# A two-layer encoder on one core: the loads, the transposes and the squares of the first twenty microseconds in another order

## The chip, the cores and the metric

The kernel runs on one core of a Trainium2 chip. The metric is the device time of one execution in microseconds. Three runs of the kernel before gave 854.73, 854.85 and 855.80 us; their median is 854.85 us.

## What is computed

The program is a trunk of two layers over one sequence of 256 tokens with 1024 channels, all in float32. A layer has two sub-layers with a residual sum after each.

```python
for layer in range(DEPTH):
    h = h + _token_mixer(_rmsnorm(h, norm1[layer]), w_in[layer], ...)   # pooling, attention, gates
    h = h + _conv_ffn(_rmsnorm(h, norm2[layer]), w_up[layer], ...)      # gated MLP
return _rmsnorm(h, norm_f)

def _rmsnorm(x, g):
    y = x * lax.rsqrt(jnp.mean(x * x, axis=-1, keepdims=True) + EPS)
    return y * g
```

The token mixer's first product is `xn @ w_in`; its columns hold among others the values `v` of three head groups, 512 columns each. The change touches only what comes before and during the product for the first 512 of these columns in the first layer.

## The kernel before, in words

**Products.** Each float32 operand is split into a high part (rounded to the multiplier's format) and a low part (the rest), and a product of two operands is made of three passes: high by high, low by high, high by low. Below, hh, lh and hl stand for these, with x's part named first and the weight's second. ScalarE makes the high part of a weight tile (`wh`), VectorE the low part (`wl`).

**The start (`begin_values_of_x`, L767 on).** x lies in the tile `h`, two tokens to a partition: t=0 holds the even tokens and t=1 the odd ones. For the values the kernel doesn't wait for the norm: the vector `norm1` is multiplied into the rows of the weights (`gcol`, one column for each chunk of 128 channels), and the factor of each token is multiplied onto the result later. So the first product needs `norm1` (loaded as 8 rows, `grows`, and turned by TensorE at L394), the raw chunks of x turned by TensorE (`turn_x`, L780 to L798), and the weights.

The contraction goes over 8 chunks of 128 channels, k=0 to 7, and there are two accumulators, t=0 and 1: 8 x 2 x 3 = 48 products (L839) in all, each 128 by 128 by 512. The weights come in two pieces of 1 MB, k=0 to 3 and k=4 to 7, the first loaded in four DMAs and the second in two. `split(k)` gives three closures that make the high part on ScalarE, the low part on VectorE, and (used for k=0 alone) the high part on VectorE (L261); `both(k)` issues the first two. The tiles for the parts of k=0 to 3 are named `m`, of k=4 and 5 `ybig`, of k=6 and 7 `at`. What `turn_x` leaves in PSUM (`xt_ps`) is cast on ScalarE to `xuh` (L793), and VectorE makes the rest `xul` (L794). `square(t, n)` sums the squares of one half of x's columns, n=0 on ScalarE (L804) and n=1 on VectorE (L808); GpSimd adds the two and raises the sum to the power -1/2 (L813 to L816), into `rstd`. `whole` (L822) adds both parts of x back together on VectorE.

**After it.** TensorE turns the two `rstd` columns into rows (`r_ps`, L908, placed behind the last of the 48 products), and goes on with the products of the next two value groups (L930), whose weights are `wh` and `wl`. From 41 us on come the long stages (L691).

**What sets the order.** Every engine works through its own list in the order in which the program's scheduler writes it; on the engines concerned this is the order of the code, save where the scheduler lets a later piece pass. SyncE issues nearly all loads. ScalarE's queue issues two DMAs at the start: `norm1` (L376) and the first quarter of x's odd tokens (L374); the other x loads and the weights are on SyncE's. Ahead of the first real work TensorE multiplies a constant tile by itself, to be busy (`warm`, widths in WARM, L37): six times 128 columns before L394, once 64 columns behind it, and once 64 columns behind the first transposes. GpSimd makes the identity for the transposes at its start.

Of the kernel before, what the change touches and what calls it, by code (L numbers as in the profile page):

```python
# [16 lines left out]
P = 128  # L17
# [16 lines left out]
NT = 5  # L34


WARM = ((P,) * 6, (P // 2,), (P // 2,))  # L37
POOLS = {("q", 1): (2, 2), ("k", 1): (0, 2)}
GROUPS = (("u", 1), ("u", 0), ("q", 0), ("k", 0), ("q", 2), ("k", 2), ("q", 1), ("k", 1))
NQ = NF // 4  # L40
# [240 lines left out]
def encoder(ctx, tc, x, w_in, w_pool, pool_scale, w_a, w_b, w_o, norm1, norm2, w_up, conv_w,  # L281
# [85 lines left out]
    def begin():  # L367


        rows8 = sm.tile([KD, P], F32, tag="gain", bufs=1, name="grows")  # L370
        first, second = W.load_by(4), W.load_by(2)

        def part_of_x(queue, t, cc):
            queue.dma_start(out=h[:, t, cc], in_=xv[:, t, cc])  # L374

        nc.scalar.dma_start(out=rows8, in_=norm1[0].rearrange("(k p) -> k p", p=P))  # L376
# [17 lines left out]
        nc.tensor.transpose(ps[:, 0:KD], rows8, ident[:KD, :KD])  # L394
        nc.vector.tensor_copy(gcol, ps[:, 0:KD])
        ps = mmp.tile([P, P], F32, tag="mm", name="warm_ps")
        warm(ps, ones, WARM[1])
        return lambda widths: warm(ps, ones, widths)

    def warm(ps, a, widths):  # L400

        for n in widths:
            nc.tensor.matmul(ps[:, 0:n], a, a[:, 0:n], start=True, stop=True)
# [363 lines left out]
    def begin_values_of_x():  # L767
# [32 lines left out]
        def square(t, n):  # L800
            cc = HALVES[n]
            junk = sm.tile([P, 512], F32, tag="p", bufs=3, name="junk")
            if n == 0:
                nc.scalar.activation(  # L804
                    junk, h[:, t, cc], AF.Square, scale=D**-0.5, accum_out=ss[t][:, n : n + 1]
                )
            else:
                nc.vector.scalar_tensor_tensor(  # L808
                    out=junk, in0=h[:, t, cc], scalar=1.0 / D, in1=h[:, t, cc],
                    op0=ALU.mult, op1=ALU.mult, accum_out=ss[t][:, n : n + 1],  # L810
                )
            if n == 0:
                nc.gpsimd.tensor_scalar_add(ss[t][:, 3:4], ss[t][:, 0:1], EPS)  # L813
            else:
                nc.gpsimd.tensor_add(out=ss[t][:, 3:4], in0=ss[t][:, 3:4], in1=ss[t][:, 1:2])
                return nc.gpsimd.tensor_tensor(out=rs[t], in0=ss[t][:, 3:4], in1=mhalf, op=ALU.pow)  # L816

        def whole(n, tag):

            ks = slice(4 * n, 4 * n + 4)  # L820
            f = big.tile([P, 4, 2, P], F32, tag=tag, name="xu")
            nc.vector.tensor_add(out=f, in0=xuh[:, ks].bitcast(F32), in1=xul[:, ks].bitcast(F32))  # L822
            return f
# [29 lines left out]
        every = ("hh", "lh", "hl")  # L853
        keep = [turn_x((t,), 0, 2) for t in range(2)]
        more(WARM[2])
        _, lo, hi = split(0)
        hi()
        for k in keep:
            k()
        lo()  # L860
        products((0, 0, ("hh",)), (1, 0, ("hh",)), (0, 0, ("lh",)), (1, 0, ("lh",)))
        keep = turn_x((0, 1), 2, 2)
        both(1)
        keep()
        products((0, 0, ("hl",)), (1, 0, ("hl",)))
        both(2)
        products((0, 1, ("hh", "lh")), (1, 1, ("hh", "lh")), (0, 1, ("hl",)), (1, 1, ("hl",)))
        both(3)
        square(0, 0)
        square(1, 0)  # L870
        square(0, 1)
        pool = square(1, 1)
        products((0, 2, ("hh", "lh")), (1, 2, ("hh", "lh")))
        keep = turn_x((0,), 4, 4)
        products((0, 2, ("hl",)), (1, 2, ("hl",)))
        keep()
        products((0, 3, every))
        keep = turn_x((1,), 4, 4)
        both(4)
        keep()  # L880
        W.load(5)
        products((1, 3, every), (0, 4, every))
        both(5)
        products((1, 4, every), (0, 5, every))
        f0 = whole(0, "q0")
        both(6)
        products((1, 5, every), (0, 6, every))
        both(7)
        products((1, 6, every), (0, 7, every))
        f1 = whole(1, "k0")  # L890
        pe = products((1, KD - 1, ("hh", "hl", "lh")))
        W.load(6)
        W.n_got = W.n_split
# [601 lines left out]
```

## Time and profile before

| what | value |
|---|---|
| median of three runs | 854.85 us |
| profiled execution, device time | 854.77 us |
| its span in the trace | 853.0 us |
| what lies around the span | 1.77 us |
| TensorE's busy time | 844.8 us of 853.0 |
| DMA | 214.03 MB, mean 251 GB/s |
| TensorE's first product of the 48 | at 5.73 us |
| TensorE's first pass of L691 | at 41.1 us |

All times inside the span count from its start. In the lists in order of time a row has the start, the length, the engine, the line, the operation, out<-in with sizes, the count of instructions that the row merges, and in brackets the idle time of that engine before it and who ended it. PE is TensorE, PEld its weight loads, DVE VectorE, ACT ScalarE, POOL GpSimd, SP SyncE; a q behind the name is the engine's queue. TensorE's matmuls overlap, so one that lasts 0.39 us can start 0.23 us behind the one before.

### The profile page before, as it was taken

How to read it: one execution, taken by the hardware profiler on the slowest of the kernel's cores; microseconds unless marked ns; L12 is line 12 of the kernel's file. 1: busy time of each engine (PE TensorE's matmuls, PEld its weight loads, DVE VectorE, ACT ScalarE, POOL GpSimd, SP SyncE). 2: the span in 40 equal slices, each digit the busy share in tenths (PEclk: the TensorE clock that was granted, in tenths of full speed). 3: DMA queues.
4: the chain of work that ended last, by engine and by line, in shares of the span. 5: the costliest groups of instructions: out<-in, count | busy, mean ns of one | idle time of the engine just before them, and what ended most of it. 6: DMA issues, size and time to landing. Idle time of an engine off the chain costs nothing.

```text
span 853.0 us, 11006 instructions
## 1 busy us (share of the span) xinstructions
PE 844.8 (99%) x3925; PEld 705.7 (83%) x3925; DVE 620.6 (73%) x885; ACT 490.5 (58%) x723; POOL 33.6 (4%) x96
## 2 busy tenths in 40 slices
PE   9999999999999999999999999999999999999997
PEld 7888888888888888888888888888888888888885
DVE  7958777757765976878655687868567767777774
ACT  7744566654543865657545454577454556556663
POOL 1700000000010000000000000000000100000000
PEclk9999999999999999999999999999999999999999
DMA  9699997895657879986726899868777489799941
GB/s 326 212 302 285 294 292 233 252 293 210 222 209 263 300 250 301 293 284 233 245 100 216 261 280 330 245 226 264 242 257 269 147 289 315 230 288 288 296 145 50
DMA packets 147678, 214.03 MB, mean 251 GB/s; under 512 B 7768, under 2 KB 68640, under 8 KB 147624
## 3 DMA queue, kind: packets, MB, share of 16 engines
q1 hardware_dynamic: 147320, 212.93, 76.8%
q8 instruction: 31, 0.51, 0.2%
q10 hardware_dynamic: 304, 0.40, 0.1%
q14 instruction: 23, 0.19, 0.1%
HBM read 186.02 MB, written 27.28 MB: 250 GB/s over the span
## 4 chain that ended last, share of the span: by engine, by line
PE 98%; DMA 1%; SPq 0%; DVE 0%; ACT 0%; issue 0%; DVEq 0%; ACTq 0%
PE t_ps L691 64%; PE v_ps L691 6%; PE res_ps L610 6%; PE res_ps L608 6%; PE res_ps L609 6%; PE v_ps L930 3%; PE pool_ps L595 1%; PE v_ps L839 1%; PE o_ps L1200 1%; PE s_ps L1152 1%; PE s_ps L1147 1%; PE o_ps L1196 1%; PE xt_ps L522 1%; DMA h<-in_x_dram 1%; PE xt_ps L787 0%; SPq L184 0%
## 5 line engine op out<-in xcount | busy, mean ns | idle before, releaser
L245 DVE TENSOR_TENSOR wl<-raw,wh 128x1024 fp32r<-128x1024 f32 x274 | 332.0, 1221 | 159.0 <-ACT wh L243 158.1
L691 PE MATMUL t_ps<-wh,x 128*128 128x512 f32 x1408 | 438.8, 390 | 0.0
L243 ACT CAST wh<-raw 128x1024 fp32r<-128x1024 f32 x274 | 286.3, 1052 | 211.5 <-PE t_ps L691 146.4
L691 PEld LDWEIGHTS t_ps<-wh,x 128*128 128x128 f32 x1408 | 264.3, 188 | 54.8
L691 PE MATMUL t_ps<-wl,x 128*128 128x512 f32 x704 | 273.9, 389 | 0.0
L691 PEld LDWEIGHTS t_ps<-wl,x 128*128 128x128 f32 x704 | 132.2, 188 | 27.3
L610 PE MATMUL res_ps<-wh,actk 128*128 128x512 f32 (+1 forms) x184 | 70.0, 380 | 0.0
L609 PE MATMUL res_ps<-wl,actq 128*128 128x512 f32 (+1 forms) x184 | 69.9, 380 | 0.0
L608 PE MATMUL res_ps<-wh,actq 128*128 128x512 f32 (+1 forms) x184 | 69.8, 380 | 0.0
L691 PE MATMUL t_ps<-wh,po 128*128 128x512 f32 x128 | 41.4, 395 | 0.0
L608 PEld LDWEIGHTS res_ps<-wh,actq 128*128 128x128 f32 x184 | 34.6, 188 | 6.6
L609 PEld LDWEIGHTS res_ps<-wl,actq 128*128 128x128 f32 x184 | 34.6, 188 | 6.6
L610 PEld LDWEIGHTS res_ps<-wh,actk 128*128 128x128 f32 x184 | 34.6, 188 | 6.6
L487 POOL TENSOR_SCALAR ss<-ss 128x1 f32<-128x1 f32 x8 | 2.2, 279 | 773.5 <-ACT junk L480 773.5
L691 PEld LDWEIGHTS t_ps<-wh,po 128*128 128x128 f32 x128 | 24.0, 188 | 4.9
L1373 ACT ACTIVATE y<-a,prm 128x256 f32<-128x256 f32 x44 | 26.5, 602 | 1.5
L608 PE MATMUL res_ps<-wh,m 128*128 128x512 f32 (+1 forms) x72 | 26.5, 368 | 0.0
L609 PE MATMUL res_ps<-wl,m 128*128 128x512 f32 (+1 forms) x72 | 26.3, 365 | 0.0
L741 DVE STREAM_TRANSPOSE crossing<-t_ps 128x512 f32<-128x512 f32 x40 | 26.2, 693 | 0.0
L610 PE MATMUL res_ps<-wh,m 128*128 128x512 f32 (+1 forms) x72 | 26.0, 366 | 0.0
L691 PE MATMUL v_ps<-wh,x 128*128 128x512 f32 x80 | 25.6, 392 | 0.0
L691 PE MATMUL t_ps<-wl,po 128*128 128x512 f32 x64 | 24.9, 390 | 0.0
(193 smaller groups left out, 931.1 us busy)
## 6 DMA issues: line engine op xcount, KB each, us to landing
raw<-in_w_in_dram SPq DMA_DIRECT2D x58, 1024.0 KB, 6.8
raw<-in_w_up_dram SPq DMA_DIRECT2D x40, 1024.0 KB, 7.1
raw<-in_w_down_dram SPq DMA_DIRECT2D x22, 1024.0 KB, 6.0
crossing<-crossing SPq DMA_DIRECT2D x22, 512.0 KB, 8.5
crossing<-way SPq DMA_DIRECT2D x16, 512.0 KB, 4.8
raw<-in_w_a_dram SPq DMA_DIRECT2D x8, 1024.0 KB, 5.1
raw<-in_w_o_dram SPq DMA_DIRECT2D x8, 1024.0 KB, 7.0
zga<-crossing SPq DMA_DIRECT2D x40, 128.0 KB, 3.7
```

Of the source, the lines that this page charges most:

```text
L243: inst = nc.scalar.copy(out=h, in_=src)
L245: inst = self.rests[i] = nc.vector.tensor_sub(out=l, in0=src, in1=h.bitcast(F32))
L522: nc.tensor.transpose(pt[:, k, :], xn[:, c0 : c0 + P], ident)
L595: nc.tensor.matmul(out, w(k), x, start=(steps is first and k == 0), stop=(steps is last and k == nk - 1), skip_group_check=turns["rest"],)
L608: nc.tensor.matmul(ps, ah, wh, start=first, stop=False, skip_group_check=on)
L609: nc.tensor.matmul(ps, ah, wl, start=False, stop=False, skip_group_check=on)
L610: nc.tensor.matmul(ps, al, wh, start=False, stop=last, skip_group_check=on)
L691: nc.tensor.matmul(ps, x2[:, 2 * n + j, part, t, :], w[:, j, :], start=(n + m == 0), stop=(n == last and m == 5),)
L741: nc.vector.transpose(out=y[:, t].rearrange("p q c j -> p c q j"), in_=rows[t])
L839: return nc.tensor.matmul(ps[t], a[:, k, t, :], w[:, k % 2, :], start=first, stop=last)
L930: nc.tensor.matmul(ps[t], a[:, k, t, :], w[:, j, :], start=(k + m == 0), stop=(k == KD - 1 and m == 2),)
L1373: nc.scalar.activation(y, a, AF.Identity, bias=b, scale=w1)
```

## The change

1. `norm1`'s 8 rows are loaded from GpSimd's queue, ahead of the identity, and no longer from ScalarE's. So the first quarter of x's odd tokens is the first DMA on ScalarE's queue.
2. The warming matmuls are seven of 128 columns before L394, none behind it, and one of 128 columns behind the first transposes.
3. The transposes of x's chunks k=2 and 3 stand behind hh and lh of k=1, and the order of the products, splits and later transposes is another.
4. All four squares are made on ScalarE, later than before: the first two behind the split of k=6, the other two behind that of k=7.

```diff
-WARM = ((P,) * 6, (P // 2,), (P // 2,))
+WARM = ((P,) * 7, (P,))
...
-        nc.scalar.dma_start(out=rows8, in_=norm1[0].rearrange("(k p) -> k p", p=P))
+        nc.gpsimd.dma_start(out=rows8, in_=norm1[0].rearrange("(k p) -> k p", p=P))
...
-        warm(ps, ones, WARM[1])
         return lambda widths: warm(ps, ones, widths)
...
-            if n == 0:
-                nc.scalar.activation(
-                    junk, h[:, t, cc], AF.Square, scale=D**-0.5, accum_out=ss[t][:, n : n + 1]
-                )
-            else:
-                nc.vector.scalar_tensor_tensor(
-                    out=junk, in0=h[:, t, cc], scalar=1.0 / D, in1=h[:, t, cc],
-                    op0=ALU.mult, op1=ALU.mult, accum_out=ss[t][:, n : n + 1],
-                )
+            nc.scalar.activation(
+                junk, h[:, t, cc], AF.Square, scale=D**-0.5, accum_out=ss[t][:, n : n + 1]
+            )
...
-        more(WARM[2])
+        more(WARM[1])
...
         products((0, 0, ("hh",)), (1, 0, ("hh",)), (0, 0, ("lh",)), (1, 0, ("lh",)))
+        both(1)
+        products((0, 1, ("hh",)), (1, 1, ("hh",)), (0, 1, ("lh",)), (1, 1, ("lh",)))
         keep = turn_x((0, 1), 2, 2)
-        both(1)
+        hi, lo, _ = split(2)
+        hi()
         keep()
-        products((0, 0, ("hl",)), (1, 0, ("hl",)))
-        both(2)
-        products((0, 1, ("hh", "lh")), (1, 1, ("hh", "lh")), (0, 1, ("hl",)), (1, 1, ("hl",)))
+        lo()
+        products((0, 0, ("hl",)), (1, 0, ("hl",)), (0, 1, ("hl",)), (1, 1, ("hl",)))
         both(3)
+        products((0, 2, ("hh",)), (1, 2, ("hh",)), (0, 3, ("hh",)), (1, 3, ("hh",)))
+        products((0, 2, ("lh",)), (1, 2, ("lh",)))
+        keep = [turn_x((0,), 4, 4)]
+        products((0, 3, ("lh",)), (1, 3, ("lh",)))
+        keep.append(turn_x((1,), 4, 4))
+        both(4)
+        W.load(5)
+        for k in keep:
+            k()
+        products(*((t, k, ("hl",)) for k in (2, 3) for t in range(2)))
+        both(5)
+        products((0, 4, every), (1, 4, every))
+        f0 = whole(0, "q0")
+        both(6)
         square(0, 0)
         square(1, 0)
+        products((0, 5, every), (1, 5, every))
+        both(7)
         square(0, 1)
         pool = square(1, 1)
-        products((0, 2, ("hh", "lh")), (1, 2, ("hh", "lh")))
...
         f1 = whole(1, "k0")
+        products((0, 6, every), (1, 6, every), (0, 7, every))
         pe = products((1, KD - 1, ("hh", "hl", "lh")))
```

TensorE's list at the start, before:

```order
L403 MATMUL gain_ps<-const-float32-1.0 128x128 x6
L394 MATMUL gain_ps<-ident,grows 128x8
L403 MATMUL warm_ps<-const-float32-1.0 128x64
L787 MATMUL xt_ps<-ident,h 128x128 x4
L403 MATMUL warm_ps<-const-float32-1.0 128x64
L839 MATMUL v_ps<-m_138,xuh 128x512 x2
L839 MATMUL v_ps<-m_138,xul 128x512 x2
L787 MATMUL xt_ps<-ident,h 128x128 x4
L839 MATMUL v_ps<-m_138,xuh 128x512 x3
```

The same place of the changed kernel, whose line numbers are one to seven lower:

```order
L402 MATMUL gain_ps<-const-float32-1.0 128x128 x7
L394 MATMUL gain_ps<-ident,grows 128x8
L786 MATMUL xt_ps<-ident,h 128x128 x4
L402 MATMUL warm_ps<-const-float32-1.0 128x128
L832 MATMUL v_ps<-m_138,xuh 128x512 x2
L832 MATMUL v_ps<-m_138,xul 128x512 x2
L832 MATMUL v_ps<-m_138,xuh 128x512 x2
L832 MATMUL v_ps<-m_138,xul 128x512 x2
L786 MATMUL xt_ps<-ident,h 128x128 x4
L832 MATMUL v_ps<-m_138,xuh 128x512 x8
```

Eight products, of k=0 and k=1, now stand ahead of the second four transposes where there were four; behind these come four hl (of k=0 and 1) and four hh (of k=2 and 3), which are the last row's eight.

ScalarE's list from its start to the next group's weights, before (`xuh` are the casts of transposes; `m`, `ybig`, `at` and `wh` the high parts of weights; `junk,ss` the squares):

```order
L376 DMA grows<-in_norm_dram 8x128
L374 DMA h<-in_x_dram 128x256
L793 ACT_TABLE_LOAD
L793 COPY xuh<-xt_ps 128x2x128 x2
L255 ACTIVATE m_138<-raw_92,gcol 128x512
L793 COPY xuh<-xt_ps 128x512
L255 ACTIVATE m_138<-raw_92,gcol 128x512 x2
L804 ACTIVATE junk,ss<-h 128x512 x2
L793 COPY xuh<-xt_ps 128x4x128
L255 ACTIVATE ybig_205<-raw_100,gcol 128x512
L793 COPY xuh<-xt_ps 128x4x128
L255 ACTIVATE ybig_205<-raw_100,gcol 128x512
```

The same of the changed kernel, up to the last square:

```order
L374 DMA h<-in_x_dram 128x256
L792 ACT_TABLE_LOAD
L792 COPY xuh<-xt_ps 128x2x128 x2
L255 ACTIVATE m_138<-raw_92,gcol 128x512 x2
L792 COPY xuh<-xt_ps 128x512
L255 ACTIVATE m_138<-raw_92,gcol 128x512
L255 ACTIVATE ybig_188<-raw_100,gcol 128x512
L792 COPY xuh<-xt_ps 128x4x128 x2
L255 ACTIVATE ybig_188<-raw_100,gcol 128x512
L255 ACTIVATE at_211<-raw_100,gcol 128x512
L802 ACTIVATE junk,ss<-h 128x512 x2
L255 ACTIVATE at_211<-raw_100,gcol 128x512
```

Behind the last row stand the other two squares, and then the next group's `wh`. The split of k=2 has passed the cast of the chunks k=2 and 3, and the squares went from behind k=3 to behind k=6 and k=7.

VectorE's list from the low parts of k=2 and 3 on, before:

```order
L256 TENSOR_SCALAR m_138<-raw_92,gcol,m_138 128x512 x2
L808 TENSOR_SCALAR junk,ss<-h 128x512 x2
L794 TENSOR_TENSOR xul<-xt_ps,xuh 128x4x128
L256 TENSOR_SCALAR ybig_205<-raw_100,gcol,ybig_205 128x512
L794 TENSOR_TENSOR xul<-xt_ps,xuh 128x4x128
L256 TENSOR_SCALAR ybig_205<-raw_100,gcol,ybig_205 128x512
```

The same place of the changed kernel:

```order
L256 TENSOR_SCALAR m_138<-raw_92,gcol,m_138 128x512 x2
L256 TENSOR_SCALAR ybig_188<-raw_100,gcol,ybig_188 128x512
L793 TENSOR_TENSOR xul<-xt_ps,xuh 128x4x128 x2
L256 TENSOR_SCALAR ybig_188<-raw_100,gcol,ybig_188 128x512
L815 TENSOR_TENSOR xu<-xuh,xul 128x1024
```

The two squares are gone from VectorE, and k=4's low part has passed the first rest of x's second half. The lists differ in a few more places up to the start of the stage of L691 (a later one of two small transposes at L418 among them); behind that no engine's list differs between the two kernels.

More of the change, by code (lines that the diff above doesn't have):

```diff
@@ L861, in begin_values_of_x @@
         products((0, 0, ("hh",)), (1, 0, ("hh",)), (0, 0, ("lh",)), (1, 0, ("lh",)))
+        both(1)
+        products((0, 1, ("hh",)), (1, 1, ("hh",)), (0, 1, ("lh",)), (1, 1, ("lh",)))
         keep = turn_x((0, 1), 2, 2)
-        both(1)
+        hi, lo, _ = split(2)
+        hi()
         keep()
-        products((0, 0, ("hl",)), (1, 0, ("hl",)))
-        both(2)
-        products((0, 1, ("hh", "lh")), (1, 1, ("hh", "lh")), (0, 1, ("hl",)), (1, 1, ("hl",)))
+        lo()
+        products((0, 0, ("hl",)), (1, 0, ("hl",)), (0, 1, ("hl",)), (1, 1, ("hl",)))
         both(3)
+        products((0, 2, ("hh",)), (1, 2, ("hh",)), (0, 3, ("hh",)), (1, 3, ("hh",)))
[12 more added lines that the diff above has]
+        both(6)
         square(0, 0)
         square(1, 0)
+        products((0, 5, every), (1, 5, every))
+        both(7)
         square(0, 1)
         pool = square(1, 1)
-        products((0, 2, ("hh", "lh")), (1, 2, ("hh", "lh")))
[L874 to L889, printed above, removed]
         f1 = whole(1, "k0")
+        products((0, 6, every), (1, 6, every), (0, 7, every))
         pe = products((1, KD - 1, ("hh", "hl", "lh")))
```

## The prediction

> **What bounds the kernel now.** I read the page first, then TensorE's waits, then the list in order of time of the first 20 us.
>
> ```profile
> span 853.0 us, 11006 instructions
> ...
> PE 844.8 (99%) x3925; PEld 705.7 (83%) x3925; DVE 620.6 (73%) x885; ACT 490.5 (58%) x723; POOL 33.6 (4%) x96
> ...
> PE 98%; DMA 1%; SPq 0%; DVE 0%; ACT 0%; issue 0%; DVEq 0%; ACTq 0%
> ```
>
> TensorE is the bound, with 98% of the chain that ended last. The list of TensorE's waits from 7.5 us to the end has one row:
>
> ```profile
> PE xt_ps L787 <- DMA h<-in_x_dram: 0.3, 1, 0.3
> ```
>
> That is the tail of the wait that ends at 7.43. Behind it TensorE waits for nothing for 840 us, so whatever the change does there shows only as the moment at which TensorE gets through the first stage. TensorE's rows of that stage:
>
> ```profile
> 0.76 2.90 PE L403 MATMUL gain_ps<-const-float32-1.0 128*128 128x128 f32 x12 [0.76 <-PEq L1477]
> 3.59 0.22 PE L394 MATMUL gain_ps<-ident,grows 8*128 8x8 f32 x1
> ...
> 4.01 0.39 PE L787 MATMUL xt_ps<-ident,h 128*128 128x128 f32 x2
> 5.21 0.44 PE L787 MATMUL xt_ps<-ident,h 128*128 128x128 f32 x2 [0.81 <-DMA h<-in_x_dram]
> ...
> 5.73 0.89 PE L839 MATMUL v_ps<-m,xuh 128*128 128x512 f32 x2
> 6.46 0.62 PE L839 MATMUL v_ps<-m,xul 128*128 128x512 f32 x2
> 7.43 0.63 PE L787 MATMUL xt_ps<-ident,h 128*128 128x128 f32 x4 [0.35 <-DMA h<-in_x_dram]
> 7.81 0.94 PE L839 MATMUL v_ps<-m,xuh 128*128 128x512 f32 x3
> ...
> 19.17 0.38 PE L908 MATMUL r_ps<-ident,rstd 128*128 128x128 f32 x2
> ```
>
> Two x loads make it wait, at 5.21 and 7.43. In the chain a stretch without a gap gives the price of a product, 11.58/51 = 0.227 us:
>
> ```profile
> 19.55 11.58 PE v_ps L930 x51
> ```
>
> All there is to win is what stands idle or warms between 3.59 and 7.43: 3.84 us, less 1.5 us of work done in them (4 products, 4 transposes, L394).
>
> **The change part by part.** ScalarE's rows:
>
> ```profile
> 0.72 0.59 ACTq L376 DMA_DIRECT2D grows<-in_norm_dram  x1
> 1.34 0.37 ACTq L374 DMA_DIRECT2D h<-in_x_dram  x1
> ...
> 5.69 0.37 ACT L793 CAST xuh<-xt_ps 128x256 fp32r<-128x256 f32 x1 [0.88 <-PE xt_ps L787]
> 6.13 0.72 ACT L255 ACTIVATE m<-raw,gcol 128x512 fp32r<-128x512 f32 x1
> 8.09 0.59 ACT L793 CAST xuh<-xt_ps 128x512 fp32r<-128x512 f32 x1 [1.24 <-PE xt_ps L787]
> 8.57 1.34 ACT L255 ACTIVATE m<-raw,gcol 128x512 fp32r<-128x512 f32 x2
> 9.81 0.62 ACT L804 ACTIVATE junk<-h 128x512 f32<-128x512 f32 x1
> 10.33 0.19 ACT L804 ACTIVATION_READ_ACCUMULATOR junk<-h 128x1 f32 x1
> ...
> 11.80 0.72 ACT L255 ACTIVATE ybig<-raw,gcol 128x512 fp32r<-128x512 f32 x1
> ```
>
> From them: a split takes 0.62 (1.34 - 0.72), a wide cast 0.48 (8.57 - 8.09), a square 0.62. VectorE's:
>
> ```profile
> 5.10 0.48 DVE L261 TENSOR_SCALAR m<-raw,gcol 128x512 fp32r<-128x512 f32 x1 [1.08 <-DMA raw<-in_w_in_dram]
> ...
> 6.10 0.42 DVE L794 TENSOR_TENSOR xul<-xt_ps,xuh 128x256 fp32r<-128x256 f32 x1 [0.18 <-ACT xuh L793]
> ...
> 12.55 0.75 DVE L256 SCALAR_TENSOR_TENSOR ybig<-raw,gcol,ybig 128x512 fp32r<-128x512 f32 x1
> 13.53 0.69 DVE L794 TENSOR_TENSOR xul<-xt_ps,xuh 128x512 fp32r<-128x512 f32 x1 [0.23 <-ACT xuh L793]
> 14.15 0.75 DVE L256 SCALAR_TENSOR_TENSOR ybig<-raw,gcol,ybig 128x512 fp32r<-128x512 f32 x1
> 14.82 1.22 DVE L822 TENSOR_TENSOR xu<-xuh,xul 128x1024 f32<-128x1024 f32 x1
> ```
>
> A low part there takes 0.67 (14.82 - 14.15), a wide rest 0.62.
>
> *x's odd tokens first.* Their DMA is issued at 0.72 instead of 1.34, so it lands up to 0.62 earlier than 5.2. The first product doesn't gain: at 5.73 it waits for VectorE's row at 5.10, which waits for the first weights. The second stands at 6.12, behind the cast that ends at 6.06; it can now follow at 5.96, and the fourth product is through near 6.65 instead of 6.92. But next comes hh of k=1, whose high part is ScalarE's row at 6.13, behind these weights' landing:
>
> ```profile
> raw<-in_w_in_dram SPq DMA_DIRECT2D x1, 256.0 KB, 4.4
> ```
>
> (issued at 1.64, landed at 6.04). It ends at 6.85, so the product starts at 6.9. The 0.27 us turn into a wait: **0**.
>
> *The transposes behind k=1.* Before, TensorE stood idle from 6.92 (6.69 + 0.23) to 7.43. Now four products run from 6.9 to 7.85, the transposes follow, and the first hl stands at 8.3 with eight products behind it, against 7.81 with four: 4 x 0.227 - 0.49 = **0.4 us won**.
>
> The price is on ScalarE: k=2's split now stands ahead of the cast of chunks 2 and 3. When k=2 lands no row tells; by 8.57 it had. The rate bounds it from below: 512 KB behind the landing at 6.04, at 347 GB/s, is 7.55.
>
> ```profile
> core 0: us, PE busy (x) PEld busy (x) DVE busy (x) ACT busy (x) POOL busy (x), PEclk, DMA share, GB/s
> 0.00:3.00 3.00, 2.24 (x10) 2.27 (x11) 0.06 (x1) 1.26 (x1) 0.69 (x6) 1.00 0.38 66
> ...
> 6.00:9.00 3.00, 2.65 (x13) 1.91 (x13) 2.04 (x4) 1.70 (x4) 0.00 (x0) 1.00 0.99 347
> 9.00:12.00 3.00, 3.00 (x16) 2.47 (x16) 3.00 (x8) 2.82 (x8) 0.91 (x3) 1.00 1.05 397
> ```
>
> I take the middle, 8.0: split 8.1, cast 8.7 to 9.3, k=3's split 9.2 to 9.92. TensorE gets to hh of k=2 at about 9.3 and waits a little, and to hh of k=3 at 9.85 and waits again: with a slower restart after each (0.1, as 6.46 - 6.12 is 0.34 and not 0.23) **0.35 lost**, from 0 (7.55) to 0.9 (8.57).
>
> *VectorE's order.* k=4's low part now stands ahead of x's rest. k=4's split starts when its 512 KB land, at 11.80 at the latest (a row without a wait). From the other side: the next 1 MB is issued at 6.12 and
>
> ```profile
> raw<-in_w_in_dram SPq DMA_DIRECT2D x1, 1024.0 KB, 9.1
> ```
>
> lands at 15.2; at 400 GB/s it and the 512 KB ahead of it take 3.9, so 11.3, which I take. Split 11.4 to 12.12, low part 12.15, rest 12.8 to 13.5; TensorE wants it at 13.4: 0.2 lost with the restart, and 0.1 for hl of k=6 behind L822. So far 0.4 - 0.35 - 0.3: **0.25 late** at the last product.
>
> *Squares.* VectorE is rid of two (1.2 us), which it spends ahead of the next group's `wl`; TensorE never waited for these, so this wins nothing. ScalarE takes two more, and all four late. Behind them are GpSimd's `rstd` and TensorE's `r_ps`, and behind `r_ps` the next group's products.
>
> ```profile
> 11.28 0.08 DVE L808 DVE_READ_ACCUMULATOR junk<-h 128x1 f32 x1
> ```
> ```profile
> 0.72 0.20 POOL masks.py:197 MEMSET ident<- 128x128 f32 x1 [0.29 <-POOLq L1477]
> 1.00 0.29 POOL masks.py:199 TENSOR_SCALAR_AFFINE_SELECT ident<-ident 128x128 f32<-128x128 f32 x1
> ...
> 11.51 0.50 POOL L815 TENSOR_TENSOR ss<-ss 128x1 f32<-128x1 f32 x1
> ...
> 13.44 0.55 POOL L816 TENSOR_TENSOR rstd<-ss,mhalf 128x1 f32<-128x1 f32 x1
> ```
>
> Before, GpSimd was done at 13.99, 5 us ahead, and 2.63 after VectorE's third square (11.36). Now ScalarE runs from 11.4: a split, two casts, two splits, two squares, a split = 6 x 0.62 + 2 x 0.48 = 4.7, third square at 16.1, done at 16.8 (0.52 + 0.19, from the rows at 9.81 and 10.33); plus 2.63 is 19.4. TensorE arrives at about 19.1. So the second `r_ps` matmul starts at 19.45 and not at 19.28; and a product of the next group that stood ahead of it (0.23) now stands behind: **0.4 late**, whether or not the 0.25 above is right, as long as that is less than the wait.
>
> *Norm's vector on GpSimd, and warming.* The trace has no DMA from GpSimd. The nearest row is the same load on ScalarE's queue: issued at 0.72 and used at 3.59 without a wait, so under 2.9 us. The seventh warm pair (2 x 0.21) moves L394 to 4.0; the transposes follow at 4.2 and 4.4, the second cast ends at 5.5. The load may come at 4.65 before anything is late: 4.65 + 0.43 (3.59 to 3.85 + 0.17) is VectorE's 5.10. GpSimd's identity behind it had 2.3 us of room. From below: 0, since nothing waits. From above: like the 256 KB above, 4.4 us, it comes at 5.1 and costs 0.45; like the 1 MB, 9.1, it comes at 9.8 and costs 5. I take 0, by the 4 KB row.
>
> Here the Trainium skill speaks against the change: "DMA: Bandwidth & Descriptors", under "Issuing engine by pattern" and "Latency and other measured facts", has loads from GpSimd built in software and slower, some 1 us to the first byte against 0.6. The trace of before has no such load to set against it. The same page, under "Anatomy of one DMA — SWDGE (gpsimd) path", gives such a DMA a fixed cost of about 2 us; by estimate the load would land near 2.8, inside the room, and the sum would stay.
>
> *Sum.* 854.77 + 0.17 + 0.23, and 0.1 for the restart behind the wait: **855.3**, about 0.4 above the median of 854.85.
>
> **The rivals.**
>
> *Earlier landings, and the squares hidden.* The first 3 us move only 66 GB/s on average; with both queues carrying x from 0.72, all loads may land up to 0.62 earlier. ScalarE's chain to `rstd` hangs on k=4's landing, so it moves with it, and TensorE's waits for splits too: 855.3 - 0.6 = 854.7, and if the waits of 0.35 go as well, 854.3. For it: the idle start. Against: SyncE's queue keeps its order, and x's and the weights' bytes share the same engines.
>
> *GpSimd's load is late* (the other side). TensorE, VectorE and ScalarE all stand behind L394; it decides from a landing at 4.65 and costs a us for each us behind. Landed at 5.85, the time is 856.5; at 7, 857.7. For it: a queue that this program has never used, and a load that shares the engines with x. Against: 4 KB, and 3.9 us of room.
>
> *No effect.* The won 0.4 holds, the later waits are half of what I take and GpSimd's chain ends just in time: 854.8.
>
> **How the numbers follow.** Forecast 855.3: 0.55 (its own range 854.9 to 855.8). Earlier landings: 0.20, of it 0.02 under 853.1. No effect: 0.12. Late load: 0.13, of it 0.10 over 856.5. A difference of 0.2%, 1.7 us, is about what a measurement of this kernel can tell from none; so faster 0.02, within 0.87, slower 0.11. The range 854.2 to 856.5 leaves out some 0.13.
>
> **What would show it.** After: hh of k=1 near 6.9 and no wait at 7.43; short waits near 9.3, 9.9 and 13.5; `r_ps` waiting for GpSimd near 19.4; L394 near 4.0. Wrong: L394 behind 4.65 with a DMA as releaser (the late load), the first 256 KB of weights used well ahead of 5.1 (earlier landings), or `r_ps` without a wait.

## The result and the profile after

The changed kernel takes 857.87 us, the median of 8 runs (857.14 to 858.51), against 855.14 for the kernel before in the same job (854.38 to 855.92, 8 runs): a ratio of 1.003 with an interval of 1.0021 to 1.0039. It is slower by 2.7 us, beyond the upper end of the predicted range. The profiled execution took 857.91 us with a span of 856.0, so 1.91 us lie around it (before 1.77).

Nearly all of the loss is there at 44 us. TensorE's first pass of L690 (L691 before) starts at 43.85 us instead of 41.15, 2.70 later; from there to the end of the span are 812.15 us (before 811.85), which is the remaining 0.3 of the two spans' difference. TensorE's waits of the changed kernel from 7.5 us on, as total, number and longest:

```profile
PE r_ps L903 <- POOL rstd L809: 1.3, 2, 1.0
PE v_ps L832 <- DVE xul L793: 0.4, 1, 0.4
PE v_ps L832 <- ACT xuh L792: 0.3, 1, 0.3
```

Before, the only row there was the tail of the wait for x at 7.43. Now there are three kinds of wait. In order of time, TensorE's rows around them:

```profile
4.66 0.20 PE L394 MATMUL gain_ps<-ident,grows 8*128 8x8 f32 x1 [0.74 <-DMA grows<-in_norm_dram]
...
5.73 0.73 PE L832 MATMUL v_ps<-m,xuh 128*128 128x512 f32 x2
...
6.81 0.74 PE L832 MATMUL v_ps<-m,xuh 128*128 128x512 f32 x2
7.38 0.62 PE L832 MATMUL v_ps<-m,xul 128*128 128x512 f32 x2
7.84 0.60 PE L786 MATMUL xt_ps<-ident,h 128*128 128x128 f32 x4
8.20 2.28 PE L832 MATMUL v_ps<-m,xuh 128*128 128x512 f32 x8
10.31 0.62 PE L832 MATMUL v_ps<-m,xul 128*128 128x512 f32 x2
...
12.04 1.18 PE L832 MATMUL v_ps<-m,xuh 128*128 128x512 f32 x4
13.51 0.49 PE L832 MATMUL v_ps<-ybig,xuh 128*128 128x512 f32 x1 [0.29 <-ACT xuh L792]
14.43 0.50 PE L832 MATMUL v_ps<-ybig,xul 128*128 128x512 f32 x1 [0.42 <-DVE xul L793]
...
19.67 0.40 PE L832 MATMUL v_ps<-at,xul 128*128 128x512 f32 x1
20.38 0.32 PE L903 MATMUL r_ps<-ident,rstd 128*128 128x128 f32 x1 [0.31 <-POOL rstd L809]
21.68 0.32 PE L903 MATMUL r_ps<-ident,rstd 128*128 128x128 f32 x1 [0.98 <-POOL rstd L809]
21.76 0.48 PE L925 MATMUL v_ps<-wh,xuh 128*128 128x512 f32 x1
```

Up to 10.31 nearly all is as predicted, save L394, which stands at 4.66 and not near 4.0. Then two late pieces at 13.5 and 14.4, and the two `r_ps` matmuls, the second at 21.68 instead of 19.28. Behind them the next group's products start. The engine that `r_ps` waits for, and the one that runs beside it, GpSimd and VectorE:

```profile
1.24 0.76 POOL L376 DMA_DIRECT2D grows<-in_norm_dram  x1 [0.81 <-POOLq L1472]
...
15.88 1.62 POOL L806 TENSOR_SCALAR ss<-ss 128x1 f32<-128x1 f32 x2 [13.28 <-ACT junk L802]
17.78 1.50 POOL L808 TENSOR_TENSOR ss<-ss 128x1 f32<-128x1 f32 x1 [0.28 <-ACT junk L802]
19.36 0.96 POOL L809 TENSOR_TENSOR rstd<-ss,mhalf 128x1 f32<-128x1 f32 x1
20.30 0.30 POOL L808 TENSOR_TENSOR ss<-ss 128x1 f32<-128x1 f32 x1
20.68 0.94 POOL L809 TENSOR_TENSOR rstd<-ss,mhalf 128x1 f32<-128x1 f32 x1
```
```profile
15.55 1.22 DVE L815 TENSOR_TENSOR xu<-xuh,xul 128x1024 f32<-128x1024 f32 x1
16.69 1.41 DVE L256 SCALAR_TENSOR_TENSOR at<-raw,gcol,at 128x512 fp32r<-128x512 f32 x2
18.01 1.21 DVE L815 TENSOR_TENSOR xu<-xuh,xul 128x1024 f32<-128x1024 f32 x1
19.15 3.39 DVE L256 SCALAR_TENSOR_TENSOR wl<-raw,gcol,wh 128x512 fp32r<-128x512 f32 x5
```

Read the two together. GpSimd's addition from 17.78 to 19.28 takes 1.50 us, for 128 numbers, and ends 0.06 behind VectorE's row that starts at 18.01 (19.22). The two additions of L808 take 1.50 and 0.30 us, where they took 0.50 and 0.73 before (L815); the power takes 0.94 to 0.96 and took 0.55 to 0.57. The four together take 3.70 us, against 2.35. ScalarE's part of the chain:

```profile
12.27 0.72 ACT L255 ACTIVATE ybig<-raw,gcol 128x512 fp32r<-128x512 f32 x1 [2.58 <-DMA raw<-in_w_in_dram]
...
16.91 0.62 ACT L802 ACTIVATE junk<-h 128x512 f32<-128x512 f32 x1
17.44 0.19 ACT L802 ACTIVATION_READ_ACCUMULATOR junk<-h 128x1 f32 x1
```

The weights of k=4 land at 12.24, not at 11.33 as before, ScalarE stands idle 2.58 us for them, and the third square is done at 17.63. GpSimd is done at 21.62 (20.68 + 0.94), 4.0 us behind it.

### The profile page after: what moved, and what is told of

It reads as the page before. It is cut to its first block, busy times and chain, and to the rows that moved or that the text cites. A ratio compares the mean times of both kernels' runs of the same rounds, so it can differ in the third digit from the quotient of the medians.

```text
span 856.0 us, 11008 instructions
## 1 busy us (share of the span) xinstructions
PE 846.0 (99%) x3925; PEld 705.7 (82%) x3925; DVE 619.4 (72%) x881; ACT 491.9 (57%) x727; POOL 34.1 (4%) x97
## 4 chain that ended last, share of the span: by engine, by line
PE 97%; ACT 1%; DMA 0%; POOL 0%; DVE 0%; issue 0%; SPq 0%; DVEq 0%; POOLq 0%; ACTq 0%
PE t_ps L690 64%; PE v_ps L690 6%; PE res_ps L609 6%; PE res_ps L607 6%; PE res_ps L608 6%; PE v_ps L925 3%; PE pool_ps L594 1%; PE o_ps L1195 1%; PE s_ps L1147 1%; PE s_ps L1142 1%; PE o_ps L1191 1%; PE xt_ps L521 1%; DMA grows<-in_norm_dram 0%; PE v_ps L832 0%; POOL rstd L809 0%
## 5 line engine op out<-in xcount | busy, mean ns | idle before, releaser
L690 PE MATMUL t_ps<-wh,x 128*128 128x512 f32 x1408 | 439.2, 390 | 0.0
L690 PEld LDWEIGHTS t_ps<-wh,x 128*128 128x128 f32 x1408 | 264.3, 188 | 54.7
L690 PE MATMUL t_ps<-wl,x 128*128 128x512 f32 x704 | 273.9, 389 | 0.0
L690 PEld LDWEIGHTS t_ps<-wl,x 128*128 128x128 f32 x704 | 132.2, 188 | 27.5
L690 PE MATMUL t_ps<-wh,po 128*128 128x512 f32 x128 | 41.4, 395 | 0.0
L690 PEld LDWEIGHTS t_ps<-wh,po 128*128 128x128 f32 x128 | 24.0, 188 | 4.9
L690 PE MATMUL v_ps<-wh,x 128*128 128x512 f32 x80 | 25.7, 392 | 0.0
L690 PE MATMUL t_ps<-wl,po 128*128 128x512 f32 x64 | 24.9, 390 | 0.0
```

Source lines behind the costliest of these rows:

```text
L690: nc.tensor.matmul(ps, x2[:, 2 * n + j, part, t, :], w[:, j, :], start=(n + m == 0), stop=(n == last and m == 5),)
```

## The experiments

Three theories stood at first: **A**, the late squares and GpSimd's stretched arithmetic; **B**, the load on GpSimd's queue; **C**, the new order itself. During the work a fourth came, **K**: TensorE's clock. Ratios are to the kernel before, run beside each of them (such a set of runs is called a job below); the intervals are 95%. k=4 is the landing of the last of the sixteen parts of that load, by the trace's record of the queues; "half" counts the products that started 427 ns apart.

| run | median us, runs | ratio | k=4 landed | first product | GpSimd done | second r_ps | half |
|---|---|---|---|---|---|---|---|
| before | 855.14, 8 | | 11.33 | 5.73 | 13.99 | 19.28 | 0 |
| after | 857.87, 8 | 1.0030 (1.0021 to 1.0039) | 12.24 | 5.73 | 21.62 | 21.68 | 0 |
| e1 norm back | 856.83, 11 | 1.0014 (1.0005 to 1.0023) | 11.47 | 6.13 | 22.03 | 22.09 | 6 |
| e3 squares alone | 857.06, 11 | 1.0019 (1.0010 to 1.0028) | 11.50 | 5.30 | 21.26 | 21.31 | 0 |
| e4 squares back | 856.79, 11 | 1.0013 (1.0004 to 1.0022) | 12.18 | 6.01 | 15.92 | 21.07 | 6 |
| e6 rows later | 856.37, 11 | 1.0009 (1.0000 to 1.0018) | 11.56 | 6.21 | 21.75 | 22.84 | 4 |
| e2 norm alone | 856.32, 11 | 1.0007 (0.9998 to 1.0016) | 12.26 | 6.39 | 14.70 | 20.90 | 3 |
| e5 order alone | 855.12, 11 | 1.0002 (0.9993 to 1.0011) | 11.32 | 6.02 | 15.56 | 20.71 | 4 |
| e7 norm behind x | 857.29, 10 | 1.0023 (1.0014 to 1.0032) | 12.45 | 5.37 | 21.84 | 21.89 | 0 |
| e8 early, ScalarE | 855.89, 11 | 1.0008 (0.9999 to 1.0017) | 12.50 | 5.16 | 13.63 | 20.37 | 0 |
| e10 before, filled | 855.12, 11 | 0.9996 (0.9987 to 1.0005) | 12.16 | 5.89 | 13.21 | 19.61 | 0 |
| e12 load ahead | 856.64, 11 | 1.0014 (1.0005 to 1.0023) | 11.36 | 6.65 | 14.30 | 19.64 | 0 |
| e13 order, filled | 855.23, 11 | 0.9995 (0.9986 to 1.0004) | 11.68 | 5.67 | 17.94 | 19.42 | 0 |
| e14 mended | 855.82, 11 | 1.0002 (0.9993 to 1.0011) | 12.34 | 6.23 | 18.60 | 20.07 | 0 |
| e15 after, filled | 857.60, 10 | 1.0027 (1.0018 to 1.0037) | 12.06 | 6.22 | 21.45 | 21.50 | 0 |
| e17 x first | 855.71, 11 | 1.0002 (0.9993 to 1.0011) | 12.00 | 5.28 | 13.95 | 19.41 | 0 |

The columns from the fourth on are of one profiled execution each, which need not be the one of the median: e1's took 858.56 us, 1.7 over its median, e5's 856.27, 1.2 over, and e12's 855.27, 1.4 under.

### One part undone, or one part alone

e1, from the changed kernel: norm's load back on ScalarE's queue, ahead of x.

```diff
-        nc.gpsimd.dma_start(out=rows8, in_=norm1[0].rearrange("(k p) -> k p", p=P))
+        nc.scalar.dma_start(out=rows8, in_=norm1[0].rearrange("(k p) -> k p", p=P))
```

> The changed kernel with the norm's vector back on ScalarE's queue, ahead of x's odd tokens. Theory A (the late squares: TensorE's two r_ps matmuls wait for GpSimd, whose small operations stretch while VectorE reads two operands from SBUF): r_ps still waits, GpSimd's operations still take 0.9 to 1.5 us each, time 857.0 to 858.2. Rival B (the load on GpSimd's queue is to blame: it delays the start, slows GpSimd's later operations or disturbs the other loads): GpSimd's operations are back at 0.5 us, time 855.0 to 855.7. Rival C (the new order of products loses by itself): 857.9, with a TensorE that waits before the r_ps.

e3, the kernel before with the squares of the change: all on ScalarE, behind the splits of k=6 and k=7.

```diff
-            if n == 0:
                 nc.scalar.activation(...)
-            else:
-                nc.vector.scalar_tensor_tensor(...)
...
         both(6)
+        square(0, 0)
+        square(1, 0)
...
         both(7)
+        square(0, 1)
+        pool = square(1, 1)
```

> The kernel before with one part of the change: all four squares on ScalarE, behind the splits of k=6 and k=7. Theory A: third square done near 16.8, GpSimd takes 3.5 to 4 us from there, so the second r_ps matmul starts at 20.4 to 20.9 instead of 19.28, and the time is 1.1 to 1.7 above before: 856.2 to 856.9. Rivals B and C: no more than 0.3 above before, since neither the load nor the order is there.

e4, the changed kernel with the squares of before (n=0 on ScalarE, n=1 on VectorE), behind the splits of k=3:

```diff
         both(3)
+        square(0, 0)
+        square(1, 0)
+        square(0, 1)
+        pool = square(1, 1)
```

> The changed kernel with the squares as they were: the first two on ScalarE, the others on VectorE, behind the split of k=3. Theory A: r_ps doesn't wait, the 1.7 us of its waits are gone: 855.6 to 856.3; what remains above before is the late landing of the second weights. Rival B: 857.2 or more, since the load is still on GpSimd's queue. Rival C: 857.2 or more.

e6, the changed kernel with `r_ps` and what hangs on it twelve products later:

```diff
+                    if (g, t, n) == (0, 0, 1):
+                        turn_rows()
```

> The changed kernel with the two r_ps matmuls (and what VectorE and ScalarE do with them) behind 12 products of the next group instead of ahead of it; squares and GpSimd's load stay. Theory A: GpSimd's chain is as late as it was (done near 21.6) but TensorE no longer stands behind it, 1.7 us less: 856.0 to 856.5. Rivals B and C: 857.5 to 858.2.

Measured 856.83, 857.06, 856.79 and 856.37. Late squares alone cost 1.4 us (857.06 against 855.62 in that job), a little over what was expected, and GpSimd's chain is again 3.75 us long (17.51 to 21.26). It is as long in e1 (18.28 to 22.03) and 4.0 us in e7 below (17.84 to 21.84): in these three nothing is loaded through GpSimd, so its load isn't what stretches the chain. e6 lies in A's range: with GpSimd done no earlier (21.75), but TensorE no longer behind it, the time falls to 856.37. But A is not all: with the squares undone (e4) 1.2 us stay, where at most 0.7 was expected, though `r_ps` no longer waits; and with norm's load undone (e1) the time falls by more than expected. The profiles of e1, e4 and e6 show something new. TensorE in e6:

```profile
4.85 0.24 PE L394 MATMUL gain_ps<-ident,grows 8*128 8x8 f32 x1 [0.76 <-DMA grows<-in_norm_dram]
5.02 1.11 PE L786 MATMUL xt_ps<-ident,h 128*128 128x128 f32 x4
5.93 0.63 PE L402 MATMUL warm_ps<-const-float32-1.0 128*128 128x128 f32 x2
6.21 1.20 PE L832 MATMUL v_ps<-m,xuh 128*128 128x512 f32 x2
7.21 1.05 PE L832 MATMUL v_ps<-m,xul 128*128 128x512 f32 x2
8.07 0.90 PE L832 MATMUL v_ps<-m,xuh 128*128 128x512 f32 x2
8.81 0.62 PE L832 MATMUL v_ps<-m,xul 128*128 128x512 f32 x2
```

Two products that last 0.62 at 8.81 last 1.05 at 7.21: they start 427 ns apart and not 230. The view by windows shows the same, and that its clock column doesn't: 6 to 9 us in the changed kernel, and then in e4, each with busy time and count of TensorE first:

```profile
6.00:9.00 3.00, 3.00 (x16) 2.33 (x15) 1.74 (x4) 1.97 (x4) 0.00 (x0) 1.00 0.88 295
```
```profile
6.00:9.00 3.00, 3.00 (x9) 2.40 (x9) 2.12 (x4) 1.68 (x3) 0.00 (x0) 1.00 0.85 251
```

Both have TensorE busy for the whole 3.00 us at a granted clock of 1.00; the one gets through 16 matmuls (four of them short transposes), the other through 9. By the spacing of the matmuls full speed is there by 3.9 to 6.0 us in 12 of the 17 traces, the changed kernel's among them, and in five (e1, e2, e4, e5, e6) only at 8.7 to 10. The Trainium skill, "TensorE: Matmul & The Clock Gate", section "What's actually happening", gives the rule: a gate lets TensorE run at half rate until one window of 3.4 us was busy, and the windows run freely, so their phase differs from run to run. The traces agree in this: half rate is 427 against 230 ns, the five late ones come at least 2.7 us behind the others, all five have an idle stretch ahead of the first products, and none of the four kernels below in which it is filled (e10, e13, e14, e15) is late. An idle stretch alone doesn't make it late: before, the changed kernel, e3 and e12 have one too, and their traces are early.

### The load, the order, and the squares early

> The kernel before with norm's load on GpSimd's queue and nothing else changed. Three theories stand: A, the squares done late on ScalarE and GpSimd's stretched arithmetic behind them delay r_ps; B, the load on GpSimd's queue is the harm, since norm's rows land at 4.5 instead of ahead of 3.6, TensorE idles there and its clock steps up later (products at 427 ns and not 230 in the first few us), and the loads behind it land later; C, the new order of products and splits itself. A and C: as before, within 0.4 us (855.2 to 856.0). B: 0.8 to 1.5 us slower than before (856.4 to 857.1), with L394 at 4.5 or later behind a DMA and the first product near 6.1 to 6.4.

e5 is e4 with e1's line as well; only the order and the warming are left.

> The changed kernel with norm's load back on ScalarE's queue ahead of x, and the squares back on their old engines, behind the splits of k=3: only the new order of transposes, splits and products is left, with the longer warming. A and B: 0.2 to 0.6 us faster than before (855.0 to 855.4), r_ps without a wait, GpSimd's last row done by 15.5. C: 0.5 to 1 us slower than before, with waits for splits near 9, 9.8 and 13.4 us that add up to it.

e7 has norm's load behind x's odd quarter on ScalarE's queue:

```diff
-        nc.gpsimd.dma_start(out=rows8, ...)
         for t, queue in enumerate((nc.sync, nc.scalar)):
             part_of_x(queue, t, slice(0, 256))
+        nc.scalar.dma_start(out=rows8, ...)
```

> The changed kernel with norm's load on ScalarE's queue behind x's odd quarter, so that x still goes first and nothing is loaded through GpSimd; squares late as in the change. A: 0.9 to 1.5 us slower than before (856.5 to 857.1), two waits of r_ps of 0.7 and 1.3 us, GpSimd's chain 3.5 to 4 us long. B: norm lands near 3.6 to 4.2, the landing of the second weights is back near 11.4, and with A's harm small the time is within 0.4 us of before. C: as slow as after, 2.5 us above before.

e8 is e7 with all four squares, still on ScalarE, behind `both(3)`.

> The kernel of the run before (norm behind x on ScalarE's queue), with all four squares on ScalarE ahead, behind the splits of k=3, where ScalarE stood idle between 9.9 and 12.2 us. A with B: both harms are gone; r_ps without a wait, GpSimd done near 16, 854.4 to 855.4, that is 0.2 to 1.2 us faster than before. C: 856 or more. If the squares delay k=4's split on ScalarE instead, a wait of TensorE at 13 to 14 us of up to 1 us, 855.6 to 856.2.

Measured 856.32, 855.12, 857.29 and 855.89. **C falls**: the order alone is 0.3 us under the 855.43 of its job, which is no difference. **B falls as it stood**: without anything on GpSimd's queue, e7 is still at 857.29, at or above where A put it, and k=4 lands at 12.45. Moving the load alone (e2) costs 0.9 us in the median, with an interval that just holds 1 and a time just under B's range; B's signs are in its profile: L394 waits until 4.60, the clock steps up late, and the first product is at 6.39. e8, with nothing late, is 1.4 us under e7 in the same job, but not under before: 855.89 is its last case, a wait of TensorE at 13 to 14 us, though not by the squares, which are done at 12.46, but by k=4, which landed at 12.50. GpSimd's rows in e8, and VectorE's beside them:

```profile
11.99 0.19 POOL L808 TENSOR_TENSOR ss<-ss 128x1 f32<-128x1 f32 x1 [0.48 <-ACT junk L802]
12.27 0.57 POOL L809 TENSOR_TENSOR rstd<-ss,mhalf 128x1 f32<-128x1 f32 x1
12.80 0.19 POOL L808 TENSOR_TENSOR ss<-ss 128x1 f32<-128x1 f32 x1
13.07 0.55 POOL L809 TENSOR_TENSOR rstd<-ss,mhalf 128x1 f32<-128x1 f32 x1
```
```profile
10.02 1.41 DVE L256 SCALAR_TENSOR_TENSOR m<-raw,gcol,m 128x512 fp32r<-128x512 f32 x2
13.29 0.75 DVE L256 SCALAR_TENSOR_TENSOR ybig<-raw,gcol,ybig 128x512 fp32r<-128x512 f32 x1 [1.86 <-ACT ybig L255]
```

VectorE idles from 11.43 to 13.29, and the same four operations take 1.50 us where they take 3.70 in the changed kernel; from the third square's end (11.84, ScalarE's read at 11.65 and its 0.19) to the last result 1.8 us pass, not 4.0.

### GpSimd's small operations measured by themselves

e11, the kernel before with a train of additions on GpSimd behind its own arithmetic:

```diff
         pool = square(1, 1)
+        for _ in range(32):
+            nc.gpsimd.tensor_scalar_add(probe, probe, EPS)
```

> The kernel before with 32 additions of 128x1 on GpSimd, one after another on a tile that nobody reads, behind the arithmetic of the squares, so from 14 us on; nothing of the computation is left out. It measures the stretch of a small GpSimd operation by itself. Theory A (GpSimd waits while VectorE works on two operands in SBUF): an addition takes 0.2 us where VectorE idles or reads PSUM, and where it runs an operation of L256, L822 or L956 with two SBUF operands, one addition lasts until within 0.1 us of that operation's end, 0.5 to 1.2 us. Otherwise: all near 0.2, or long ones that start and end anyhow. The time as before, 854.4 to 856.4, since GpSimd's next work is wanted at 25 us.

The group of the 32 additions (min, median and max in ns); then, by windows, the length of two stretches, VectorE's busy time on that tile (none) and GpSimd's with the count; then VectorE's rows of these stretches:

```profile
L876 POOL TENSOR_SCALAR probe<-probe x32: 209/578/1050, 13.9 to 31.2; 128x1 f32<-128x1 f32 x32
```
```profile
18.60:23.90 5.30, 0.00 (x0) 4.64 (x8) 1.00 0.98 317
23.90:25.40 1.50, 0.00 (x0) 1.05 (x5) 1.00 0.36 64
```
```profile
18.41 5.38 DVE L256 SCALAR_TENSOR_TENSOR wl<-raw,gcol,wh 128x512 fp32r<-128x512 f32 x8
23.71 1.65 DVE L916 SCALAR_TENSOR_TENSOR xu<-xu,gcol,r_ps 128x256 f32<-128x256 f32 x4
```

Beside L256, which reads two operands from SBUF, an addition takes 4.64/8 = 0.58 us, one for each of VectorE's operations, and each ends 0.07 behind it. Beside L916, whose second operand lies in PSUM, it takes 1.05/5 = 0.21, and nothing ends with anything. That is A's mechanism as it was expected. The Trainium skill has the rule in "SBUF — State Buffer", section "Who interferes with whom": a VectorE instruction with two SBUF inputs contends with a GpSimd instruction that reads SBUF, since they share a pair of ports that one of them locks, and the order of issue decides which one waits. The rows agree. The time of this run, 859.05, missed: TensorE waited 2.0 us for VectorE at 120.6 us and ran at half rate for 3 us behind that wait. Only the train's rows are used here; why that wait came stayed open. e17's trace has a smaller one, 0.6 us at 297 us, behind another VectorE operation (L1400), and no other trace has one anywhere behind 23 us.

### The clock's step, and a load of its own

e10, the kernel before with TensorE's idle stretch filled; e13 is e5 with two such products, and all squares on ScalarE, two behind `both(3)` and two behind `both(5)`.

```diff
-        keep = [turn_x((t,), 0, 2) for t in range(2)]
+        keep = [turn_x((0,), 0, 2)]
+        more((P,) * 3)
+        keep.append(turn_x((1,), 0, 2))
```

> The kernel before with three more warming products between the transposes of x's even and of its odd tokens, where TensorE stands idle from 4.2 to 5.2 us. Theory K: TensorE's clock steps up at a moment that differs from execution to execution, and an idle stretch ahead of the first products lets the step slip by some 3 us; of 65 runs of before 27 lie in 854.4 to 855.1 and 38 in 855.3 to 856.4, which are these two cases, and the changed kernel's idle stretch from 3.9 to 4.65 makes the later step the usual one. K: nearly all runs within 854.4 to 855.2, median near 854.8, so 0.5 us faster than before, with products at 230 ns from the first one on. If the two groups have another cause, both stay, and the median is as before (855.2 to 855.7).

> The new order alone (norm and x loaded as before), with two more warming products in TensorE's idle stretch ahead of x's odd tokens, and all four squares on ScalarE, two behind the splits of k=3 and two behind those of k=5. Theory K and A: with the clock up from the first products and VectorE free for x's last low parts the wait near 13 to 14 us goes, GpSimd is done near 17.5 to 18.8, ahead of r_ps, 854.2 to 855.0. If the squares delay the splits of k=6, or r_ps waits for GpSimd, 855.2 to 856.5. Without K: two groups of runs a us apart.

e12 is e2 with a load that nobody reads in the old place of norm's:

```diff
+        nc.scalar.dma_start(out=spare, in_=norm1[0].rearrange("(k p) -> k p", p=P))
         nc.gpsimd.dma_start(out=rows8, in_=norm1[0].rearrange("(k p) -> k p", p=P))
```

> The kernel with norm on GpSimd's queue alone, and a spare 4 KB load of the same rows, which nobody reads, on ScalarE's queue ahead of x's odd quarter, so that x's odd tokens are issued at 1.34 again and norm still comes through GpSimd. In every run so far in which x's odd quarter was issued at 0.72 but one the weights of k=4 landed at 12.2 to 12.4, in those with 1.34 at 11.3 to 11.5. If x's earlier issue does that, k=4 lands at 11.3 to 11.6 here; if GpSimd's queue does it, at 12.2 or later. The time: norm still lands near 4.5, so the later step of the clock stays the usual one, 856.0 to 856.6, at most 0.2 us better than with norm moved alone.

**K holds in the main.** All 11 runs of e10 lie in 854.74 to 855.63 and all 11 of e13 in 854.86 to 855.47, while the 27 runs of before in this job spread over 854.29 to 856.92, 13 of them above 855.63. The upper group is gone. That the upper group was at half rate for longer is inferred, since no execution of it was traced. The medians gain less than K gave, 0.46 and 0.35 us, and both intervals hold 1, so neither gain is clear of noise; the filling itself makes the first product a little later when the clock had been up anyway (e10 5.89 against 5.73). e13 missed its 854.2 to 855.0: `r_ps` doesn't wait, but a wait of 0.4 us for VectorE stayed at 13.9. e12's k=4 lands at 11.36, as was expected of x's issue time, though norm came through GpSimd; its time was no better than e2's. Norm landed later than expected there, at 5.26, and L394 waited until 5.40.

### What is left

e14 is the changed kernel with the squares two and two behind k=3 and k=5 and `WARM = ((P,) * 9, (P,))`; e15 has only that line; e17 is the kernel before with only e7's edit.

> The changed kernel with norm still on GpSimd's queue and x's odd tokens still first, but with two more warming pairs ahead of L394, where TensorE stood idle from 3.9 to 4.65 us, and the squares, all on ScalarE, two behind the splits of k=3 and two behind those of k=5. If the late squares and the clock are the whole loss, it falls to where the new order with idle stretch filled was: 854.9 to 855.5, some 2.4 us under the changed kernel, with k=4 landing anywhere between 11.4 and 12.5. If x's earlier issue costs something by the later landing of k=4, 855.6 to 856.3, with a wait of TensorE at 13 to 14 us of over 0.6 us. If GpSimd's load itself costs more, above 856.3.

> The changed kernel with nothing but two more warming pairs ahead of L394, where it stood idle from 3.9 to 4.65 us. Theory A says that behind the late squares TensorE waits for r_ps anyway, until GpSimd is done at 21.6, so that a faster start only makes these waits longer: 857.3 to 858.3, as the changed kernel, with the waits of r_ps together 2.0 us or more. If the clock's late step was a part of the loss by itself, 856.3 to 857.0.

> The kernel before with one thing changed: norm's load stands behind x's odd quarter on ScalarE's queue and not ahead of it, so x's odd tokens go out at 0.72 and nothing goes through GpSimd. If the earlier issue makes the weights of k=4 land later (12.2 to 12.5 in five of six runs with 0.72, 11.3 to 11.7 in six of eight with 1.34), they land at 12.2 or later here too, and what the first products gain (they start at 5.2 to 5.4) is lost at 13 to 14 us: 855.0 to 856.0, no faster than before. If not, k=4 lands near 11.4 and the time is 854.3 to 855.0, with TensorE's idle stretch before the first products nearly gone and the clock's early step in most runs.

Measured 855.82, 857.60 and 855.71. e15 against e14 is the cleanest price of the late squares, in one job with all else the same: 1.8 us. TensorE's waits, of e15 and then of e14:

```profile
PE r_ps L903 <- POOL rstd L809: 1.3, 2, 1.0
PE v_ps L832 <- DVE xul L793: 0.4, 1, 0.4
```
```profile
PE v_ps L832 <- DVE xul L793: 0.4, 1, 0.4
```

GpSimd's chain is stretched in e14 too, 3.3 us from the third square (15.27) to the last result (18.60), but it ends ahead of TensorE, which comes to `r_ps` at 19.96. e15 can't be told from the changed kernel (1.0027 against 1.0030, with intervals that overlap), as A expected. Two things qualify this: the changed kernel's own trace has no product at half rate, and the waits for `r_ps`, expected to reach 2.0 us, stayed at 1.3, with the first product at 6.22 there and not at 5.73. e14 is not distinguishable from before; its time lies in the second of its ranges, but its wait at 14.5 us is 0.4 and not over 0.6.

The two parts add up. Each against the kernel before of its own job, the changed kernel is 2.7 us slower, e4 (squares undone) 1.2, e1 (load and x's order undone) 1.2, and e5 (both undone) is 0.3 faster. So either one undone gives back 1.5 us, and both together 3.0, as far as medians can tell that are uncertain by some 0.8 us each. By which way the load's 1.5 us come while the squares are late stays open: e1's one trace is of its slowest run.

x's odd quarter first: issued at 0.72, k=4 lands at 11.56 to 12.50 in nine traces (median 12.24, eight at 12.0 or later; e17 itself at 12.00, short of the 12.2 expected); issued at 1.34, at 11.32 to 12.16 in eight (median 11.5, seven under 12.0; the eighth is e10). So the earlier issue goes with a later landing of k=4 by some 0.7 us, but not in every execution, and by itself it costs nothing that can be measured (e17). In the new order with the squares early it may cost some: e8 and e14, with k=4 at 12.50 and 12.34, are 0.5 and 0.3 us over before, e5 and e13, at 11.32 and 11.68, 0.3 and 0.35 under, but none of the four is clear of noise. Why the earlier issue goes with the later landing was not settled: the sixteen parts of that load end between 10.39 and 12.24 in the changed kernel, and between 10.18 and 11.33 before, so it is the last of them and not the first that is late.

## Why the prediction was wrong, point by point

**x's odd tokens first: 0, right in this trace.** x's odd tokens landed at 3.43 and not at 5.17, 1.74 us earlier, where I had allowed 0.62. The first product stays at 5.73, as forecast, but for another reason. The first weights landed 0.65 us earlier (4.34 by the queues' record, against 4.99); this was part of the rival of earlier landings. L394 ate it: it waited for norm until 4.66, and VectorE's first row came at 5.09 as before.

**GpSimd's load: 0, at the edge.** 4.66 against the 4.65 from which it was said to cost, with a DMA as releaser: by the letter my sign of the late load, but by 0.01 us. The row of issues:

```profile
grows<-in_norm_dram POOLq DMA_DIRECT2D x1, 4.0 KB, 3.3
```

It took 3.3 us from issue to landing, over the 2.9 that I took from ScalarE's row. The 2.8 estimated from the Trainium skill's "DMA: Bandwidth & Descriptors" (a landing near 2.8, issued at 1.24 it would be 3.2) is passed too: it landed at 4.52. The price I set on a late landing, a us for each us, wasn't tested by the changed kernel; in e12, where L394 stood 0.75 behind 4.65, the first product came 0.92 later than before and the stage of L691 only 0.35 (41.50). What I missed is a second price, that an idle TensorE can let the step of its clock slip (e2). In the changed kernel's own trace it did not slip.

**Transposes behind k=1: 0.4 won, right.** hh of k=1 at 6.81 (6.9 forecast), transposes at 7.84 (7.85), hl at 8.20 (8.3).

**Splits of k=2 and 3: 0.35 lost, right.** The eight products from 8.20 to 10.31 take 2.11 us, 0.29 over 8 x 0.227.

**VectorE's order: 0.2 + 0.1, too small.** The two waits leave 0.69 and 0.92 us between products (from 12.82, with the products before 0.23 apart), so 1.15 over. About half goes with the order: with k=4 at 11.68, e13 still has 0.78 between these products (13.08 and 13.86), 0.55 over. The rest goes with the landing at 12.24 where I took 11.3.

**Squares: 0.4, the step that failed.** I wrote: third square at 16.1, done at 16.8, "plus 2.63 is 19.4". It was done at 17.63, 0.83 later, as ScalarE's chain hangs on k=4's landing; and GpSimd needed 4.0 us and not 2.63, 1.37 more. Together 21.6, and the 0.4 became 2.4. The 2.63 was read from one place and carried to another where VectorE has other work: in the earlier place it idled or read PSUM for part of the time, in the new one it runs L815 and L256 without a gap. The rows of before held the sign already, and I took them as the operation's own length: additions of 0.50 and 0.73 where two others took 0.21.

```profile
10.61 0.21 POOL L813 TENSOR_SCALAR ss<-ss 128x1 f32<-128x1 f32 x1 [9.32 <-ACT junk L804]
11.22 0.21 POOL L813 TENSOR_SCALAR ss<-ss 128x1 f32<-128x1 f32 x1 [0.40 <-ACT junk L804]
11.51 0.50 POOL L815 TENSOR_TENSOR ss<-ss 128x1 f32<-128x1 f32 x1
12.09 0.57 POOL L816 TENSOR_TENSOR rstd<-ss,mhalf 128x1 f32<-128x1 f32 x1
12.63 0.73 POOL L815 TENSOR_TENSOR ss<-ss 128x1 f32<-128x1 f32 x1
```

**The sum.** Forecast +0.5; measured 2.70 at 41 us: the 0.4 and 0.35 as forecast, 0.85 more at 13 to 14 us, most of which only makes TensorE's wait for `r_ps` shorter, and GpSimd's 21.62 setting the end. Had its chain taken e8's 1.8 us, it would have been done at 19.4, before TensorE gets there (19.9: the last product starts at 19.67); so the stretch and the landing stand together, and the stretch is the larger. This is worked out from traces; no run has late squares without the stretch.

**The rivals.** Late load at 7 gives 857.7, near the result, by a mechanism that did not happen. No rival had the stretch in it. The sign that I named, `r_ps` waiting for GpSimd near 19.4, was the right place to look.

## What to carry to other kernels

An operation's length on GpSimd is no constant: before moving its work, look at what VectorE does beside it in the new place, and whether those operations read two operands from SBUF. Small arithmetic that an end hangs on belongs early: the four squares behind k=3 and k=5 instead of k=6 and k=7 gave back 1.8 us, though GpSimd's chain was still stretched there, because it ended before TensorE came to it. Where VectorE idles, the chain is short as well (1.8 us in e8). And when a change adds idle time ahead of TensorE's first products, look at the distance between products, and in more than one execution: the late step of the clock came in five of the seventeen traces, and the times of the kernel before fell into two groups.

## What the runs showed of the hardware

A TensorE that is busy throughout at a granted clock of 1.00 can still be at half rate; the count of matmuls in a window tells it, the busy share doesn't (16 against 9). Filling the idle stretch ahead of the first products took away the slower of the two groups of runs that the kernel before had. And a load is landed with the last of its sixteen parts: for k=4 it came 1.15 us behind the first before and 1.85 in the changed kernel, at nearly the same mean rate of all loads up to 11.33 us (264 and 258 GB/s).
